# Forget-gate attention: two heads on two halves of TensorE's rows, values token-major, PE's order in blocks

## The chip, the cores and the metric

One core of a Trainium2 chip runs the whole program in one launch. The metric is the device time of an execution in microseconds. Engines: PE (TensorE) multiplies matrices, DVE (VectorE), ACT (ScalarE) and POOL (GpSimd) work on elements, SP (SyncE) issues most DMAs.

## What is computed

Three transformer layers follow each other on 1024 tokens of width 1024: an attention layer with two kinds of heads, the forget-gate layer that this change is about, and a layer with a gated recurrence, cross attention and experts. Of the forget-gate layer, with 16 heads of width 64:

```python
def fox_layer(x, g_in, w_in, b_f, w_out):
    h = rms_norm(x, g_in)
    q, k, v, f_logit, gate = split_cols(h @ w_in, ODD_SPLITS)   # 1024, 1024, 1024, 16, 1024
    log_cum = jnp.cumsum(jax.nn.log_sigmoid(f_logit + b_f), axis=1)
    o = causal_block_attention(q, k, v, log_cum=log_cum)        # 16 heads of 64
    return x + (o * jax.nn.silu(gate)) @ w_out
# in the attention, for each block of 128 queries:
#   s = q k^T / 8 + log_cum[t] - log_cum[s], masked causally; softmax over s; p @ v
```

All is float32.

## The kernel before

Float32 operands of a projection or a score are split into a high part `hi` in a reduced format (F32R) and the rest `lo`; a product is three matmuls (`mm3`, lines 338 to 343: hi hi, hi lo, lo hi). Transposes and value products run on plain float32.

The forget-gate layer (`fox`, lines 1191 to 1377) works on eight pairs of heads; a pair's 128 columns fill the partitions. `prep(p)` makes the filler units of pair p: a unit is 24 matmuls of 512 tokens with a weight block as stationary operand, two units each for queries, keys, gate, and from pair 2 on values. Values of pairs 0 and 1 are made token-major ahead of the loop (line 1203); those of pairs 2 to 7 come out with features on the partitions, and eight transposes turn each pair's into tokens (lines 1266 to 1278).

Scores: for each head, queries are stored with `hi` on the head's 64 partitions and `lo` on the other 64, and the keys' `hi` and `lo` are each stored twice, on both halves; the copies between halves are DMAs on ACT's queue (lines 1256, 1257). So one matmul over 128 partitions is (hi + lo) times a key part, and two passes make a score.

The attention itself (`causal_attn`, lines 579 to 656) has three stages for each of the 64 (pair, block) tiles n: `soft` (scores into a PSUM bank `ps`, bias and running minimum on DVE in line 600, exponential on ACT in line 606, normalisation on POOL in line 609), `tr` (transposes of P into `pt` banks, copied to `PT` by ACT in line 630) and `pv` (line 644: values as stationary operand, 64 columns, one head on each half of the array's columns and of the PSUM partitions). `pipeline` emits in step t the stages `soft(t+2)`, `tr(t+1)`, `pv(t-2)` and one filler unit, interleaved piece by piece; a few `order` edges keep PE's order near that. Within this, a scheduler that simulates the engines orders the instructions of every engine but SP, whose queue is in program order. In the last pair the filler is the memory projections of a later layer (`k.mem.fill`, line 1902), from step 58 on.

PSUM has eight banks: three `ps` (scores), two `pd` (projections), two `pt` (transposes), one `po` (value products). Most tiles of SBUF come out of 41 slots of 128x1024 float32.

Of the kernel before, what the change touches and what calls it, by code (L numbers as in the profile page):

```python
# [66 lines left out]
ET = mybir.EngineType  # L67
SW_MAN = {ET.SP, ET.PE, ET.DVE, ET.Activation, ET.Pool}
# [30 lines left out]
def prep(inp):  # L99
    a = {k: np.asarray(v) for k, v in inp.items()}  # L100
    A = {}
# [475 lines left out]


def causal_attn(k, st, n, qk, bias, scale, val, done):


    nc = k.nc
    P, PT, po = {}, {}, {}

    def soft(i):
        w = (i + 1) * 128
        for a in range(2):
            sb = k.slot([128, 1024], name="P")
            acc = 1e30
            for c in range(0, w, 512):  # L590
                m = min(512, w - c)
                ps = k.pss()
                passes = qk(a, i, c, m)
                for t, (l, r) in enumerate(passes):
                    ins = nc.tensor.matmul(ps[:, :m], l, r, start=t == 0, stop=t == len(passes) - 1)  # L595
                    if t == 0 and c == 0:
                        k.order(ins, st.get(("T", n + i - 2)))
                for c0, n0, b in bias(a, i, c, m):
                    mx = k.small([128, 1], "m", bufs=12)
                    nc.vector.tensor_tensor_reduce(sb[:, c0:c0 + n0], ps[:, c0 - c:c0 - c + n0], b,  # L600
                                                   -scale, acc, OP.add, OP.min, mx)
                    acc = mx
                if c + 512 < w:
                    yield
            sm = k.small([128, 1], "sum", bufs=8)
            nc.scalar.activation(sb[:, :w], sb[:, :w], AF.Exp, bias=acc, scale=-1.0, accum_out=sm)  # L606
            ri = k.small([128, 1], "rinv", bufs=8)
            nc.vector.reciprocal(ri, sm)  # L608
            nc.gpsimd.tensor_scalar(sb[:, :w], sb[:, :w], ri, 0.0, op0=OP.mult, op1=OP.add)  # L609
            P[i, a] = sb  # L610
            yield

    def tr(i):
        for a in range(2):
            p = P.pop((i, a))
            for c in range(0, i + 1, 4):
                m, q = min(4, i + 1 - c), (i // 2, a, c // 4)
                if q not in PT:
                    PT[q] = k.slot([128, 4, 256], name="PT")
                pt = k.pst()  # L620
                for j in range(m):
                    ins = nc.tensor.transpose(pt[:, j * 128:(j + 1) * 128], p[:, (c + j) * 128:(c + j + 1) * 128],  # L622
                                              k.ident)
                    if a == 0 and c == 0 and j == 0:
                        k.order(ins, st.get(("V", n + i - 2)))
                    st["T", n + i] = ins
                dst = PT[q][:, :m, i % 2 * 128:(i % 2 + 1) * 128]
                src = pt[:, :m * 128].rearrange("p (j n) -> p j n", j=m)
                if (a + c // 4) % 4 < 3:
                    nc.scalar.copy(dst, src)  # L630
                else:
                    nc.vector.tensor_copy(dst, src)
                yield

    def pv(i):
        if i % 4 == 0:
            po[0] = k.pso()
        o, half = po[0], i // 2 + 1
        last = half * 2 - 1
        for j in range(i % 2 * half, (i % 2 + 1) * half):  # L640
            n0 = 128 if j == last else 0
            cols = slice((last - 1) % 4 * 128 + n0, (last % 4 + 1) * 128)
            for a in range(2):
                st["V", n + i] = nc.tensor.matmul(o[a * 64:(a + 1) * 64, cols], val(a, j),  # L644
                                                  PT[i // 2, a, j // 4][:, j % 4, n0:],
                                                  start=j == 0, stop=j == last)
            if j % 4 == 3 or j == last:
                for a in range(2):
                    PT.pop((i // 2, a, j // 4))
            if j % 2:  # L650
                yield
        if i % 4 == 3:
            done(i // 4, o)
        yield

    return soft, tr, pv
# [534 lines left out]
def fox(k, ft, resid, after_tile):  # L1191
# [42 lines left out]
    st, qk, gt, lcb, vt = {}, {}, {}, {}, {}  # L1234
    god = k.dram([8, 128, 1024], "god")

    def prep(p):
        def q_evac(half, ps):
            cols = slice(half * 512, (half + 1) * 512)
            if half == 0:  # L1240
                qk[p] = [[k.slot([128, 1024], F32R, name="st") for _ in range(2)] for _ in range(3)]
            for a in range(2):
                r, o = slice(a * 64, a * 64 + 64), slice(64 - a * 64, 128 - a * 64)
                q = qk[p][0][a]
                nc.scalar.activation(q[r, cols], ps[r, :], AF.Copy, scale=0.125)
                nc.vector.scalar_tensor_tensor(q[o, cols], ps[r, :], 0.125, q[r, cols].bitcast(F32),  # L1246
                                               op0=OP.mult, op1=OP.subtract)

        def k_evac(half, ps):
            cols = slice(half * 512, (half + 1) * 512)  # L1250
            for a in range(2):
                r, o = slice(a * 64, a * 64 + 64), slice(64 - a * 64, 128 - a * 64)
                h, l = qk[p][1][a], qk[p][2][a]
                nc.scalar.copy(h[r, cols], ps[r, :])
                nc.vector.tensor_sub(l[r, cols], ps[r, :], h[r, cols].bitcast(F32))
                k.q.dma_start(out=h[o, cols].bitcast(F32), in_=h[r, cols].bitcast(F32))
                k.q.dma_start(out=l[o, cols].bitcast(F32), in_=l[r, cols].bitcast(F32))
# [8 lines left out]
        def v_evac(half, ps):  # L1266
            if half == 0:
                vt[p] = k.slot([128, 1024], name="vT")
            nc.scalar.copy(vt[p][:, half * 512:(half + 1) * 512], ps)
            if half == 1:  # L1270
                v = V[p] = k.slot([128, 8, 128], name="V")
                for b in range(2):
                    pt = k.pst()
                    for t in range(4):
                        i = b * 4 + t
                        nc.tensor.transpose(pt[:, t * 128:(t + 1) * 128], vt[p][:, i * 128:(i + 1) * 128], k.ident)
                    nc.vector.tensor_copy(v[:, b * 4:(b + 1) * 4, :].rearrange("p a b -> p (a b)"), pt)
                vt.pop(p)

# [5 lines left out]
        ev = [q_evac, k_evac] + ([v_evac] if p >= 2 else []) + [g_evac]  # L1285
        units = []
        for e, i in zip(ev, k.fc[p]):
            units += k.proj_units(ft, i, e, order=st.get(("V", (p - 1) * 8 - 1)))
# [6 lines left out]
    def passes(p):  # L1295
        def f(a, i, c, n):
            qs, h, l = qk[p][0][a], qk[p][1][a], qk[p][2][a]
            q = qs[:, i * 128:(i + 1) * 128]
            return [(q, h[:, c:c + n]), (q, l[:, c:c + n])]
        return f  # L1300

    def bias(p):
        def f(a, i, c, n):
            out = []
            if min(c + n, i * 128) > c:
                out.append((c, min(c + n, i * 128) - c, lcb[p][a][:, c:min(c + n, i * 128)]))
            if c + n == (i + 1) * 128:
                dm = k.small([128, 128], "dm", bufs=3)
                nc.gpsimd.tensor_add(dm, lcb[p][a][:, i * 128:(i + 1) * 128], k.mask)  # L1309
                out.append((i * 128, 128, dm))  # L1310
            return out
        return f

    def val(p):
        if p < 2:
            return lambda a, j: V[0][j // 4][:, j % 4, p * 128 + a * 64:p * 128 + (a + 1) * 64]
        return lambda a, j: V[p][:, j, a * 64:(a + 1) * 64]

    def done(p):
        def f(half, o):  # L1320
            t = k.slot([128, 512], name="go")
            nc.vector.scalar_tensor_tensor(t, o, 0.5, gt[p][:, half * 512:(half + 1) * 512], op0=OP.mult, op1=OP.mult)
            k.q.dma_start(out=god[p, :, half * 512:(half + 1) * 512], in_=t)
        return f
# [7 lines left out]
    def fill(t):  # L1332
        p, i = divmod(t, 8)
        if p >= 7:
            return k.mem.fill(FOX_FILL, t) + [ahead(t - 56)]
        if t < 0:
            return []
# [1601 lines left out]
```

## Time and profile before

| | us |
|---|---|
| three runs, median (lowest to highest) | 2300.29 (2298.59 to 2302.42) |
| the profiled execution | 2301.81 |
| its span | 2300.0 |
| the forget-gate stage in it | about 583 to 1203 |

Times in the profile are microseconds from the span's start unless marked ns. PE is the matmul row and PEld the weight-load row of TensorE; records of matmuls overlap, since each shows its whole way through the array. PEclk is the granted TensorE clock as a share of full speed (2.4 GHz). A releaser behind `<-` is what ended an idle time.

### The profile page before, as it was taken

How to read it: one execution, taken by the hardware profiler on the slowest of the kernel's cores; microseconds unless marked ns; L12 is line 12 of the kernel's file. 1: busy time of each engine (PE TensorE's matmuls, PEld its weight loads, DVE VectorE, ACT ScalarE, POOL GpSimd, SP SyncE). 2: the span in 40 equal slices, each digit the busy share in tenths (PEclk: the TensorE clock that was granted, in tenths of full speed). 3: DMA queues.
4: the chain of work that ended last, by engine and by line, in shares of the span. 5: the costliest groups of instructions: out<-in, count | busy, mean ns of one | idle time of the engine just before them, and what ended most of it. 6: DMA issues, size and time to landing. Idle time of an engine off the chain costs nothing.

```text
span 2300.0 us, 32867 instructions
## 1 busy us (share of the span) xinstructions
PE 2211.1 (96%) x12164; PEld 1757.5 (76%) x12164; DVE 1184.4 (51%) x2892; ACT 960.0 (42%) x2018; POOL 452.6 (20%) x620
## 2 busy tenths in 40 slices
PE   7999999999999999999999999999899999899797
PEld 7888778888877777777788789787577888666564
DVE  6322678834344443444344332687445637766544
ACT  5322667823344444444442221355202122557453
POOL 2000455400122222222310010121001102222121
PEclk9999999999999999999999999999999999999898
DMA  4112221233222211221254221326656124778774
GB/s 165 37 48 99 81 58 38 75 118 104 75 69 72 63 55 60 74 60 56 83 174 147 103 91 47 106 69 216 233 220 259 69 106 176 263 235 293 226 216 165
DMA packets 96515, 282.06 MB, mean 123 GB/s; under 512 B 11980, under 2 KB 25036, under 8 KB 96352
## 3 DMA queue, kind: packets, MB, share of 16 engines
q1 hardware_dynamic: 75616, 225.32, 28.4%
q0 software_dynamic: 6624, 24.12, 4.4%
q10 hardware_dynamic: 14112, 30.48, 4.2%
q8 instruction: 97, 1.59, 0.3%
q14 instruction: 66, 0.54, 0.1%
HBM read 202.73 MB, written 65.62 MB: 117 GB/s over the span
## 4 chain that ended last, share of the span: by engine, by line
PE 85%; DVE 6%; DMA 4%; ACT 3%; issue 2%; SPq 0%; POOL 0%; ACTq 0%; POOLq 0%; DVEq 0%
PE pd L340 15%; PE pd L342 15%; PE pd L341 15%; PE ps L340 4%; PE po L644 4%; PE ps L342 4%; PE ps L341 4%; PE ps L595 3%; PE pt L622 3%; PE pd L2538 2%; PE pd L1902 2%; PE ps L990 2%; PE po L1033 1%; PE pt L1019 1%; PE ps L2562 1%
## 5 line engine op out<-in xcount | busy, mean ns | idle before, releaser
L340 PE MATMUL pd<-fh,wh 128*128 128x512 f32 x880 | 353.5, 402 | 0.6 <-DVE st L1246 0.3
L342 PE MATMUL pd<-fh,wl 128*128 128x512 f32 x880 | 347.9, 395 | 0.5 <-DVE wl L318 0.5
L341 PE MATMUL pd<-fl,wh 128*128 128x512 f32 x880 | 347.4, 395 | 0.0
L340 PE MATMUL pd<-wh,fh 128*128 128x258 f32 (+3 forms) x616 | 203.2, 330 | 2.4 <-DVE n L1436 2.4
L342 PE MATMUL pd<-wh,fl 128*128 128x258 f32 (+3 forms) x616 | 200.9, 326 | 0.0
L341 PE MATMUL pd<-wl,fh 128*128 128x258 f32 (+3 forms) x616 | 200.8, 326 | 0.0
L340 PEld LDWEIGHTS pd<-fh,wh 128*128 128x128 f32 x880 | 165.2, 188 | 43.0 <-issue 7.1
L342 PEld LDWEIGHTS pd<-fh,wl 128*128 128x128 f32 x880 | 165.2, 188 | 40.1 <-issue 2.3
L341 PEld LDWEIGHTS pd<-fl,wh 128*128 128x128 f32 x880 | 165.5, 188 | 34.9 <-issue 0.2
L318 DVE TENSOR_TENSOR wl<-w,wh 128x1024 fp32r<-128x1024 f32 (+5 forms) x92 | 106.8, 1166 | 138.3 <-ACT wh L316 138.3
L316 ACT CAST wh<-w 128x1024 fp32r<-128x1024 f32 (+5 forms) x99 | 97.3, 989 | 139.3 <-PE pd L341 108.2
L630 ACT COPY PT<-pt 128x512 f32<-128x512 f32 (+2 forms) x192 | 86.4, 478 | 139.9 <-PE pt L622 139.4
L609 POOL TENSOR_SCALAR P<-P,rinv 128x256 f32<-128x256 f32 (+7 forms) x128 | 96.1, 751 | 192.3 <-DVE rinv L608 163.3
L606 ACT ACTIVATE P<-P,m 128x256 f32<-128x256 f32 (+7 forms) x128 | 99.6, 778 | 76.7 <-DVE m L600 75.8
L340 PEld LDWEIGHTS pd<-wh,fh 128*128 128x128 f32 x616 | 116.4, 189 | 14.2 <-DVE n L1436 2.8
L341 PEld LDWEIGHTS pd<-wl,fh 128*128 128x128 f32 x616 | 116.3, 189 | 10.6 <-issue 1.0
L342 PEld LDWEIGHTS pd<-wh,fl 128*128 128x128 f32 x616 | 116.3, 189 | 10.2 <-issue 0.2
L1309 POOL TENSOR_TENSOR dm<-lcb,mask 128x128 f32<-128x128 f32 x128 | 60.7, 474 | 282.4 <-DVE m L600 226.3
L595 PE MATMUL ps<-st,st 128*128 128x512 f32 (+3 forms) x384 | 106.9, 372 | 1.2 <-DMA st<-st 0.8
L644 PE MATMUL po<-PT,V 128*64 128x256 f32 (+1 forms) x640 | 96.4, 373 | 0.0
L2420 DVE TENSOR_TENSOR ml<-mw,mh 128x1024 fp32r<-128x1024 f32 x66 | 80.1, 1226 | 29.8 <-ACT mh L2417 15.4
L622 PE MATMUL pt<-ident,P 128*128 128x128 f32 x576 | 88.7, 276 | 2.6 <-POOL P L609 2.4
(513 smaller groups left out, 4721.9 us busy)
## 6 DMA issues: line engine op xcount, KB each, us to landing
mw<-w_moe SPq DMA_DIRECT2D x70, 512.0 KB
w<-o_wc SPq DMA_DIRECT2D x30, 512.0 KB
w<-w_moe SPq DMA_DIRECT2D x26, 512.0 KB
xr<-xs SPq DMA_DIRECT2D x18, 512.0 KB
s<-x_wkv SPq DMA_DIRECT2D x16, 512.0 KB
lcb<-dn SPq DMA_DIRECT2D x16, 512.0 KB
st<-st ACTq DMA_DIRECT2D x64, 128.0 KB
wkd<-kvw SPq DMA_DIRECT2D x32, 256.0 KB
```

The costliest lines, as they stand in the source:

```text
L316: nc.scalar.copy(hi[:, :n], raw[:, :n])
L318: (eng or nc.vector).tensor_sub(lo[:, :n], raw[:, :n], hi[:, :n].bitcast(F32))
L340: first = mm(out, lhs[0], rhs[0], start=start, stop=False)
L341: mm(out, lhs[0], rhs[1], start=False, stop=False)
L342: mm(out, lhs[1], rhs[0], start=False, stop=stop)
L595: ins = nc.tensor.matmul(ps[:, :m], l, r, start=t == 0, stop=t == len(passes) - 1)
L606: nc.scalar.activation(sb[:, :w], sb[:, :w], AF.Exp, bias=acc, scale=-1.0, accum_out=sm)
L609: nc.gpsimd.tensor_scalar(sb[:, :w], sb[:, :w], ri, 0.0, op0=OP.mult, op1=OP.add)
L622: ins = nc.tensor.transpose(pt[:, j * 128:(j + 1) * 128], p[:, (c + j) * 128:(c + j + 1) * 128], k.ident)
L630: nc.scalar.copy(dst, src)
L644: st["V", n + i] = nc.tensor.matmul(o[a * 64:(a + 1) * 64, cols], val(a, j), PT[i // 2, a, j // 4][:, j % 4, n0:], start=j == 0, stop=j == ...
L2420: nc.vector.tensor_sub(W[c][1], raw[c], W[c][0].bitcast(F32))
```

## The change

- Scores: queries and keys keep `hi` and `lo` as whole 128-partition tiles (four tiles for a pair). A score is three passes (hi hi, hi lo, lo hi) on a head's 64 partitions; the passes of the pair's two heads alternate, one on the upper and one on the lower half of the rows, into different PSUM banks. The copies between halves go. A second chunk of the second head takes a `pd` bank.
- Values of pairs 2 to 7 are made token-major too: for two pairs at a time, 256 weight columns as moving operand, `v_unit` with 48 matmuls for two token blocks; four such units for each two pairs, as filler in steps 6 and 7 of pairs 0 to 5. Their transposes go. The weights of a group stay in slots.
- `causal_attn` goes; in the loop PE is in program order too (`FOX_MAN`): per step the value products of tile t-2, the scores of tile t+2, the transposes of tile t+1, then the filler. The other engines' instructions for the softmax stand behind the transposes in the program.

```diff
+FOX_MAN = {ET.SP, ET.PE}
...
+    A["o_wv2"] = np.stack([v[:, c * 256:(c + 1) * 256].reshape(8, 128, 256).transpose(1, 0, 2).reshape(128, 2048) for c in range(1, 4)])
...
-        ch += [q[:, c], kk[:, c]] + ([v[:, c]] if p >= 2 else []) + [gate[:, c]]
+        ch += [q[:, c], kk[:, c], gate[:, c]]
...
         def q_evac(half, ps):
             cols = slice(half * 512, (half + 1) * 512)
             if half == 0:
-                qk[p] = [[k.slot([128, 1024], F32R, name="st") for _ in range(2)] for _ in range(3)]
-            for a in range(2):
-                r, o = slice(a * 64, a * 64 + 64), slice(64 - a * 64, 128 - a * 64)
-                q = qk[p][0][a]
-                nc.scalar.activation(q[r, cols], ps[r, :], AF.Copy, scale=0.125)
-                nc.vector.scalar_tensor_tensor(q[o, cols], ps[r, :], 0.125, q[r, cols].bitcast(F32),
-                                               op0=OP.mult, op1=OP.subtract)
+                qk[p] = [k.slot([128, 1024], F32R, name="qk") for _ in range(4)]
+            h, l = qk[p][:2]
+            nc.scalar.activation(h[:, cols], ps, AF.Copy, scale=0.125)
+            nc.vector.scalar_tensor_tensor(l[:, cols], ps, 0.125, h[:, cols].bitcast(F32), op0=OP.mult, op1=OP.subtract)
...
+    def v_unit(g, x):
+
+        if x % 2 == 0:
+            V.setdefault(g, []).append(k.slot([128, 4, 256], name="V"))
+        ps = k.psd()
+        for t in range(2):
+            for kt in range(8):
+                wh, wl = WV[g][kt // 4]
+                c = slice(kt % 4 * 256, (kt % 4 + 1) * 256)
+                k.mm3(ps[:, t * 256:(t + 1) * 256], ft.stat(2 * x + t, kt), (wh[:, c], wl[:, c]), kt == 0, kt == 7)
+        nc.scalar.copy(V[g][x // 2][:, x % 2 * 2:x % 2 * 2 + 2, :].rearrange("p a b -> p (a b)"), ps)
...
+    def score(n):
+
+        p, i = divmod(n, 8)
+        w = (i + 1) * 128
+        qh, ql, kh, kl = qk[p]
+        ps = {}
+        for c in range(0, w, 512):
+            m = min(512, w - c)
+            for a in range(2):
+                ps[c, a] = k.psd() if c and a else k.pss()
+            for l, r in ((qh, kh), (qh, kl), (ql, kh)):
+                for a in range(2):
+                    h = slice(a * 64, a * 64 + 64)
+                    nc.tensor.matmul(ps[c, a][:, :m], l[h, i * 128:w], r[h, c:c + m], start=l is qh and r is kh, stop=l is ql)
...
+    def turn(n):
+        i, z = n % 8, n // 2
+        for a in range(2):
+            p = P.pop((n, a))
+            for c in range(0, i + 1, 4):
+                m, q = min(4, i + 1 - c), (z, a, c // 4)
+                if q not in PT:
+                    PT[q] = k.slot([128, 4, 256], name="PT")
+                pt = k.pst()
+                for j in range(m):
+                    nc.tensor.transpose(pt[:, j * 128:(j + 1) * 128], p[:, (c + j) * 128:(c + j + 1) * 128], k.ident)
...
+                if (a + c // 4) % 4 < 3:
+                    nc.scalar.copy(dst, src)
...
+            g = p // 2 + 1
+            if p < 6:
+                units[p] += [lambda x=x: v_unit(g, x + p % 2 * 2) for x in range(2)]
+                if p % 2 == 0:
+                    units[p][4] = lambda u=units[p][4]: (u(), v_weights(g))
...
-    pipeline(64, [run(0), run(1), run(2)], FOX_SKEW, fill)
-    for t in range(8 - min(FOX_SKEW), 12):
+    a, b, c = FOX_SKEW
+    with k.tc.manual_schedule(engines=FOX_MAN):
+        for t in range(-a, 64 - c):
+            if 0 <= t + c:
+                outs(t + c)
+            if t + a < 64:
+                score(t + a)
+            if 0 <= t + b < 64:
+                turn(t + b)
+            if t + a < 64:
+                soft(t + a)
+            if t < 64:
+                fill(t)
+            else:
+                weave([ahead(t - 56)])
```

`outs` is the value product of `pv` with the same loops, `soft` the exponential, reciprocal and normalisation as before.

## Rows read from the trace of the kernel before

**Rows 1.** The page: busy time, share of the span and instructions of each engine.

```profile
PE 2211.1 (96%) x12164; PEld 1757.5 (76%) x12164; DVE 1184.4 (51%) x2892; ACT 960.0 (42%) x2018; POOL 452.6 (20%) x620
```

**Rows 2.** Windows: stretch, length, busy us per engine (instructions), PEclk, DMA share, GB/s.

```profile
583.00:1203.00 620.00, 615.95 (x3255) 470.48 (x3253) 266.83 (x865) 282.20 (x587) 156.25 (x256) 1.00 0.25 77
1120.00:1160.00 40.00, 37.90 (x226) 27.65 (x226) 17.06 (x68) 19.01 (x45) 12.88 (x23) 0.96 0.28 96
```

**Rows 3.** Matmuls in 583:1203 by line and shape: count | busy us, mean ns.

```profile
L340 PE MATMUL pd<-fh,wh 128*128 128x512 f32 x480 | 192.7, 401 | 0.3 <-DVE st L1246 0.3
...
L622 PE MATMUL pt<-ident,P 128*128 128x128 f32 x576 | 88.7, 276 | 2.6 <-POOL P L609 2.4 <-ACT PT L630 0.2
L644 PE MATMUL po<-PT,V 128*64 128x256 f32 x512 | 82.6, 395 | 0.0
L595 PE MATMUL ps<-st,st 128*128 128x512 f32 x192 | 63.6, 421 | 0.3 <-DVE m L600 0.3
L1902 PE MATMUL pd<-s,s 128*128 128x256 f32 x128 | 28.9, 380 | 0.0
L644 PE MATMUL po<-PT,V 128*64 128x128 f32 x128 | 21.6, 286 | 0.0
L595 PE MATMUL ps<-st,st 128*128 128x384 f32 x64 | 18.3, 368 | 0.0
L595 PE MATMUL ps<-st,st 128*128 128x256 f32 x64 | 14.8, 314 | 0.0
L595 PE MATMUL ps<-st,st 128*128 128x128 f32 x64 | 14.1, 285 | 0.9 <-DMA st<-st 0.8
L1276 PE MATMUL pt<-ident,vT 128*128 128x128 f32 x48 | 7.2, 272 | 0.0
L340 PE MATMUL ps<-wh,fh 128*128 128x512 f32 x8 | 3.3, 417 | 0.0
...
```

**Rows 4.** Timeline of PE: start us, length us, instruction, records merged.

```profile
905.26 0.39 PE L341 MATMUL pd<-fl,wh 128*128 128x512 f32 x1
...
906.19 0.40 PE L342 MATMUL pd<-fh,wl 128*128 128x512 f32 x1
...
909.64 1.04 PE L622 MATMUL pt<-ident,P 128*128 128x128 f32 x8
```

**Rows 5.** Timeline of PE in a later layer, projections of 258 columns.

```profile
1400.05 0.28 PE L340 MATMUL pd<-wh,fh 128*128 128x258 f32 x1
...
1400.90 0.28 PE L341 MATMUL pd<-wl,fh 128*128 128x258 f32 x1
```

**Rows 6.** Timeline of the weight loads, whole array and column halves.

```profile
902.06 0.30 PEld L595 LDWEIGHTS ps<-st,st 128*128 128x128 f32 x2 [0.38 <-DVE rinv L608]
902.43 0.20 PEld L644 LDWEIGHTS po<-PT,V 128*64 128x64 f32 x4
```

**Rows 7.** Timeline of PE around value products, at two places.

```profile
923.68 0.62 PE L595 MATMUL ps<-st,st 128*128 128x512 f32 x2
924.24 0.86 PE L644 MATMUL po<-PT,V 128*64 128x256 f32 x6
...
650.88 1.08 PE L644 MATMUL po<-PT,V 128*64 128x256 f32 x8
651.89 0.51 PE L595 MATMUL ps<-st,st 128*128 128x256 f32 x2
```

**Rows 8.** Timeline: transposes in a row and the copies out of their banks.

```profile
1131.62 1.09 PE L622 MATMUL pt<-ident,P 128*128 128x128 f32 x8
...
1132.31 1.07 ACT L630 COPY PT<-pt 128x512 f32<-128x512 f32 x2
...
1133.04 0.63 PE L622 MATMUL pt<-ident,P 128*128 128x128 f32 x4 [0.33 <-POOL P L609]
...
1176.97 0.96 PE L622 MATMUL pt<-ident,P 128*128 128x128 f32 x7 [0.20 <-ACT PT L630]
```

**Rows 9.** The page's costliest groups: the exponential.

```profile
L606 ACT ACTIVATE P<-P,m 128x256 f32<-128x256 f32 (+7 forms) x128 | 99.6, 778 | 76.7 <-DVE m L600 75.8
```

More of the change, by code (lines that the diff above doesn't have):

```diff
@@ L576, in run @@
         return max(t.values())
[L579 to L586, printed above, removed]
-        for a in range(2):
[L588 to L656, printed above, removed]
@@ L1264, in l_load @@
                 lcb[p].append(t)
[L1266 to L1278, printed above, removed]
         def g_evac(half, ps):
@@ L1283, in g_evac @@
             k.silu2(gt[p][:, half * 512:(half + 1) * 512], ps)
-        ev = [q_evac, k_evac] + ([v_evac] if p >= 2 else []) + [g_evac]
         units = []
-        for e, i in zip(ev, k.fc[p]):
-            units += k.proj_units(ft, i, e, order=st.get(("V", (p - 1) * 8 - 1)))
+        for e, i in zip([q_evac, k_evac, g_evac], k.fc[p]):
+            units += k.proj_units(ft, i, e)
         if p == 0:
@@ new lines, in val @@
+    def val(p, a, j):
+        c = p % 2 * 128 + a * 64
+        return V[p // 2][j // 4][:, j % 4, c:c + 64]
+    def score(n):
[12 more added lines that the diff above has]
+        for a in range(2):
+            P[n, a] = k.slot([128, 1024], name="P")
+            dm = k.small([128, 128], "dm", bufs=3)
+            nc.gpsimd.tensor_add(dm, lcb[p][a][:, i * 128:w], k.mask)
+            M[n, a] = 1e30
+            for c in range(0, w, 512):
+                m = min(512, w - c)
+                for c0, c1, b in ((c, min(c + m, w - 128), lcb[p][a]), (w - 128, c + m, dm)):
+                    if c1 <= c0:
+                        continue
+                    mx = k.small([128, 1], "m", bufs=12)
+                    nc.vector.tensor_tensor_reduce(P[n, a][:, c0:c1], ps[c, a][:, c0 - c:c1 - c], b if b is dm else b[:, c0:c1],
+                                                   -1.0, M[n, a], OP.add, OP.min, mx)
+                    M[n, a] = mx
@@ new lines, in outs @@
+    def outs(n):
+        p, i = divmod(n, 8)
+        if i % 4 == 0:
+            po[0] = k.pso()
+        o, half = po[0], i // 2 + 1
+        last = half * 2 - 1
+        for j in range(i % 2 * half, (i % 2 + 1) * half):
+            n0 = 128 if j == last else 0
+            cols = slice((last - 1) % 4 * 128 + n0, (last % 4 + 1) * 128)
+            for a in range(2):
+                nc.tensor.matmul(o[a * 64:(a + 1) * 64, cols], val(p, a, j), PT[n // 2, a, j // 4][:, j % 4, n0:],
+                                 start=j == 0, stop=j == last)
+            if j % 4 == 3 or j == last:
+                for a in range(2):
+                    PT.pop((n // 2, a, j // 4))
+        if i % 4 == 3:
@@ L1364, in ahead @@
                     yield
[L1366 to L1367 removed]
+    a, b, c = FOX_SKEW
[11 more added lines that the diff above has]
+                fill(t)
+            else:
+                weave([ahead(t - 56)])
+    for t in range(8 - c, 12):
         for _ in ahead(t):
```

82 lines of the change are left out of this document (33 added, 49 removed).

## The prediction

> **What bounds the kernel now.** Read the page's busy shares first: TensorE (PE) is busy 96% of the span, the next engine 51% [rows 1]. Then the windows over the stage that the change rewrites, from the first query projection of the forget-gate layer to the first output projection after its last value product: 620.0 us long, PE busy 615.95, granted clock 1.00, DMA 25% busy, VectorE (DVE) 267 us and ScalarE (ACT) 282 us busy [rows 2]. So in this stage time is what PE's instructions take one after another, and an edit is worth what it takes off PE's row; DVE, ACT and DMA work counts only where PE ends up waiting for it.
>
> How much of the 620 is arithmetic? The counts of each shape are in [rows 3]; "busy" there overlaps (a matmul's record lasts longer than its turn on the array), so I price by start-to-start distance. Projections of 512 columns: four apart in 0.93 us, 0.2325 each; transposes: eight in 1.04 with the last record's 0.27 taken off, 0.110 each [rows 4]. A 258-column matmul: seven apart in 0.85, 0.121 [rows 5]; I use it for 256 columns, and midway, 0.176, for 384. Weight loads: two in 0.30, each 0.19 long, so they start 0.11 apart; a 128-column score can't go faster than its load, 0.109 [rows 6]. Value products of two heads lie side by side on the two column halves: eight records in 1.08, less the last record's 0.38 and a first load of 0.05, are three distances for four pairs, 0.216 a pair of 256 columns [rows 7]. The sums:
> - projections 3 x 480 x 0.2325 = 334.8, and 22 of the output projection that the scheduler already put here, 5.1
> - transposes (576 + 48) x 0.110 = 68.6
> - value products 256 pairs x 0.216 + 64 x 0.108 = 62.2
> - scores 192 x 0.2325 + 64 x (0.176 + 0.121 + 0.109) = 70.6
> - the memory projections (L1902) 128 x 0.216 = 27.6
>
> Together 568.9. The other 51.1 us are the loss. 4.05 is idle PE (620.0 less 615.95). Most of the rest is changing between the whole array and column halves. Two 512-column scores ahead of a value block take 0.56 where 0.465 is due: 0.09 to enter. Eight records take 1.01 to the next instruction where 0.865 is due: 0.146 inside and on leaving. The next matmul then waits for its load, 0.107 [rows 6, 7]. One visit costs 0.34, the timeline of the stage has 100 of them (650.88 and 924.24 are two), so 34. The last 13 are blocks in which one head stands alone, and a clock dip.
>
> **The change, part by part.**
>
> *Scores.* Per chunk and pair of heads: before, two heads x two passes, four matmuls on 128 rows; after, three passes x two heads on 64 rows each, in adjacent instructions and separate PSUM banks. If the halves run side by side as the column halves do, a chunk costs three turns and not four: 70.6 x 3/4 = 52.9, a gain of 17.6. No 64-row matmul is in the trace. Bounds: 17.6 gained, or, if the halves take turns, six turns for four, 35.3 lost. I take the gain, by the nearest row: in column mode four weight loads fit in 0.20 at 0.13 each [rows 6], and the value blocks run at a pair per 0.216 [rows 7].
>
> *Values token-major.* Out: 12 units x 24 x 0.2325 and 48 transposes x 0.110, 72.2. In: 12 units x 48 matmuls of 256 columns x 0.121 = 69.7. Gain 2.5. Between the 256-column price and the 258-column row there is hardly room: 1 either way.
>
> *PE's order by mode.* Each step now is value products, scores, transposes, filler, so three mode changes: into columns 0.09, inside and out 0.146, load for the rows 0.107, out of the rows 0.095 and first transpose 0.055 (as for columns), 0.49 a step, 64 steps, 31.4. It replaces the whole 51.1. The rows show the price for columns only; for rows it may be nothing (0.15 a step less) or a little more.
> The Trainium skill (TensorEngine Tiling (Array Packing), Key Properties) says that changing the tiling mode drains TensorE and changing the tile within a mode does not. By it all three changes cost, and the sum stands; the trace agrees for whole-array to column changes (0.34 a visit) and can't speak of rows.
>
> *New waits, because PE's order is fixed.* Before, the scheduler put projections between the transposes of a tile; after, all transposes of a tile stand together, and scores, filler and everything else on PE queue behind them. From the fifth tile of a pair on there are four groups (4 + m of the first head, then the second), only two PSUM banks, and every copy out of them is on ACT. Eight transposes start at 1131.62, the first copy at 1132.31, the third group at 1133.04: 1.42 later, 1.36 without the slow first one; 0.73 after the copy began, which is one copy and 0.14. That row names POOL as releaser, but the row at 1176.97 shows the same wait with ACT's copy named [rows 8]. The first two groups fill 0.55, 0.66, 0.77 and 0.88 (m = 1 to 4, 0.110 each), so PE waits 0.81, 0.70, 0.59, 0.48: 2.58 a pair of heads, 20.6 in eight pairs. Bounds: 10 if half is hidden, 50 if copies come late (a rival below).
>
> *Steps without filler.* In 1120 to 1160, where before's filler ran out for two steps, PE idles 2.10 and the clock falls to 0.96 of 40 us, 1.6 more [rows 2]. After, the value units sit in pairs 0 to 5, so two more steps lack filler, and at the start the first transposes wait for the first softmax with nothing between: I put 7.6 (twice 3.7, rounded up) in place of it. Other small waits: 3, a guess between 0 and 10.
>
> *Costed at nothing:* the 64-row splits on ACT and DVE become half as many 128-row ones, 64 small copies between halves and their issues on ACT's queue go, 12 copies of value transposes go; all lay behind PE. The value weights come as six slot pieces instead of six of the 30 blocks on SP's queue, the same bytes; at 25% DMA they stay hidden. The row broadcasts keep their place in SP's queue. Without PE as cover the weight splits would show: that happens only in the steps just priced. The 22 output-projection matmuls can't be drawn forward any more and come later, which the sum holds as 5.1 on both sides.
>
> *Sum for the stage:* 568.9 - 17.6 - 2.5 + 31.4 + 20.6 + 7.6 + 3 = 611.4, against 620.0: 8.6 less. The profiled execution took 2301.81 us (1.8 more than its span); the median of the runs is 2300.29, 1.5 lower. 2301.8 - 8.6 - 1.5 = 2292.
>
> **The rivals.**
>
> (a) *The row halves cost no drain.* 0.15 x 64 = 9.6 less: 2282. For it: transposes and projections follow each other with no loss, so not every change of shape costs. Against: the column change does.
>
> (b) *The two halves share their weight load.* Each pair then lasts at least two loads, 0.215: +0.039, +0.094, +0.106 for 384, 256 and 128 columns, x 3 passes x 2 chunks x 8 = 11.5 more: 2303.5, no change. For it: whole-array loads stand 0.11 apart; against: column loads go side by side [rows 6].
> The Trainium skill (TensorE: Matmul & The Clock Gate, Part 3: Packing small matmuls, Measured speedup vs the span model) reports 3.07 times, not 4, for four strips of rows at 512 columns. An estimate from that page: two halves gain 1.54, not 2, scores come to 68.8 and the time to 2308. No run here shows it yet.
>
> (c) *The halves don't run together at all*, so the change doesn't do what it says. 52.9 more than forecast: 2345, slower. It decides from where a pair costs more than 1.16 turns (8.6 of 52.9). Against it stand the column pairs.
>
> (d) *Copies behind exponentials.* PE can't go round a late copy now. An exponential takes 0.78 on ACT [rows 9]. If in half of the 64 steps one stands ahead of the first copy, 32 x 0.78 = 25 more: 2317, slower. It decides from twelve such steps on. For it: ACT is in order and its order was not fixed by hand. Against it: the copies stand before the exponentials in the program, and ACT is under half busy.
>
> **How the numbers follow.** Forecast 0.48 (own range 2283 to 2303), (a) 0.12, (b) 0.15, (c) 0.08, (d) 0.17. Runs of this kernel lie within 0.2%, about 4.6 us, of each other; a smaller change can't be told. Faster (below 2295.7): 0.35 out of the forecast's 0.48, all of (a), 0.01 of (b): 0.48. Same: 0.13 of the forecast and 0.08 of (b): 0.21. Slower: (c), (d) and the last 0.06 of (b): 0.31. The range for 8 in 10 runs from 2277 (a with fewer small waits) to 2325 (d and 8 us of small waits), and leaves out (c) and the far side of (d).
>
> **What would show it right or wrong.** Scores: adjacent 64-row records of the two heads starting within 0.01 us, pairs 0.23 apart at 512 columns; (b) shows as 0.215 at 128 columns, (c) as 0.23 between heads. Values: 0.121 a matmul. Modes: three losses of 0.09 to 0.15 in each step, 64 value blocks and not 100. Banks: PE idle 0.5 to 0.8 before the third group of transposes of tiles 5 to 8 of a pair, released by ACT's copy; (d) shows as idles over 1 us with an exponential between. Idle in the stage should go from 4 to about 30 us while PE's arithmetic falls by 20. A stage under 600 or over 625 us would mean that one of these terms is not as I have it; PE waiting for POOL's normalised tiles in steps with filler would mean a wait that I left out.

## The result, and the profile after

The changed kernel took 2317.81 us (2315.77 to 2318.90, four runs) against 2299.86 for the kernel before beside it (2298.59 to 2302.42, four): a ratio of 1.0076, 95% interval 1.0058 to 1.0093. The change costs 0.8%, 18 us; the forecast was 9 us less. The profiled execution took 2315.77, its span 2314.0, 14.0 more than before's.

The page's busy shares, to be read beside [rows 1]:

```profile
PE 2190.0 (95%) x12596; PEld 1750.0 (76%) x12596; DVE 1152.9 (50%) x2848; ACT 940.6 (41%) x1986; POOL 451.7 (20%) x620
```

PE does 21 us less work and DVE and ACT 31.5 and 19.4 less, yet the time is longer. Windows over the rewritten stage and inside it (columns as in [rows 2]):

```profile
582.00:1220.00 638.00, 599.51 (x3705) 467.05 (x3704) 234.68 (x820) 261.02 (x553) 152.98 (x256) 0.98 0.18 62
...
670.00:674.80 4.80, 0.10 (x1) 0.00 (x0) 4.17 (x11) 1.62 (x3) 0.00 (x0) 0.99 0.67 211
674.80:678.00 3.20, 3.15 (x11) 2.88 (x12) 1.57 (x5) 2.26 (x4) 0.00 (x0) 0.50 0.97 351
```

From its first projection (582.3) to the first output projection after its last value product (1219.8) the stage lasts 637.6, against 620.2. PE's busy time fell by 16 [rows 2]; its idle time rose from 4 to 38.5. The lower lines show one such place: PE stands still for almost 5 us, and in the 3.2 us behind that its granted clock is 0.50, the lower of its two levels (1.2 GHz). Who made it wait, summed over the stage (line waited for, us in total, times, longest):

```profile
PE pt L1265 <- ACT PT L1269: 28.6, 30, 4.8
PE ps L342 <- DVE m L1242: 6.1, 1, 6.1
PE pt L1265 <- POOL P L1253: 3.5, 3, 2.6
```

Transposes (L1265) waited for ScalarE's copies out of their banks (L1269). The 30 waits are of two kinds: 27 of 0.33 to 0.71 us, and three of 4.75. This is the first of the three, in pair 0: PE's timeline, then that of ScalarE, of VectorE and of the load queue (ACTq and SPq issue DMAs):

```profile
666.40 0.40 PE L344 MATMUL pd<-fh,wl 128*128 128x512 f32 x1
666.73 0.87 PE L1283 MATMUL po<-PT,V 128*64 128x256 f32 x8
667.53 1.20 PE L1230 MATMUL ps<-qk,qk 64*128 64x512 f32 x7
...
668.57 0.39 PE L1230 MATMUL ps<-qk,qk 64*128 64x512 f32 x1
668.57 0.39 PE L1230 MATMUL pd<-qk,qk 64*128 64x512 f32 x1
668.80 0.38 PE L1230 MATMUL ps<-qk,qk 64*128 64x512 f32 x1
668.80 0.38 PE L1230 MATMUL pd<-qk,qk 64*128 64x512 f32 x1
669.12 0.98 PE L1265 MATMUL pt<-ident,P 128*128 128x128 f32 x7
674.85 1.73 PE L1265 MATMUL pt<-ident,P 128*128 128x128 f32 x7 [4.75 <-ACT PT L1269]
676.23 0.78 PE L342 MATMUL pd<-fh,wh 128*128 128x512 f32 x1
...
678.34 0.40 PE L344 MATMUL pd<-fh,wl 128*128 128x512 f32 x1
```

```profile
667.39 1.99 ACT L318 CAST wh<-w 128x1024 fp32r<-128x1024 f32 x2
671.45 0.34 ACTq L1292 DMA_DIRECT2D god<-go  x1
673.17 1.04 ACT L318 CAST wh<-w 128x1024 fp32r<-128x1024 f32 x1 [3.80 <-DMA w<-o_wc]
674.13 0.96 ACT L1269 COPY PT<-pt 128x512 f32<-128x512 f32 x2
```

```profile
668.46 2.36 DVE L320 TENSOR_TENSOR wl<-w,wh 128x1024 fp32r<-128x1024 f32 x2 [0.25 <-ACT wh L318]
670.74 0.68 DVE L1291 SCALAR_TENSOR_TENSOR go<-po,gt 128x512 f32<-128x512 f32 x1
```

```profile
669.71 1.46 SPq L282 DMA_DIRECT2D w<-o_wc  x2
```

The first bank could be copied from about 669.9 on (0.75 after its first transpose, as in the rows at 728.53 and 729.28 below). But ScalarE, which works in the order of its queue, had two things ahead of the copies. One is the store of the gated output, which waits for VectorE; VectorE had first to split two value weights (668.46 to 670.7), so the store goes out at 671.45. The other is the cast of a query weight that only the *next* pair's filler needs: its load could be issued at 669.71 only, when the first split had freed a raw buffer (there are two), and landed at 673.17. The copies start at 674.13. PE, whose order is fixed, has a filler that is ready and may not take it up. The same happens in pairs 2 and 4, the other two in which value weights are split.

What was forecast of PE's own work can be read in the same lines. The two heads' matmuls start together (668.57 and 668.57; 285 pairs of records are 3 ns apart in the median) and pairs follow each other 0.23 apart.

The Trainium skill (TensorE: Matmul & The Clock Gate, Part 3: Packing small matmuls, Measured speedup vs the span model) has 3.07 times for four strips of rows, from which I had estimated 1.54 for two halves. This trace doesn't bear that estimate out: at 512 columns a pair of halves takes the 0.23 of one whole matmul.

Into columns: 0.33 from 666.40 to 666.73 where 0.23 is due. Inside and out of columns: 0.80 to 667.53 where 0.65 is due (two pairs at 0.216, two of half the columns). In and out of rows: 1.59 for six pairs to 669.12 where 1.40 is due. Together 0.44 a step; 0.49 was forecast.

The counts, beside [rows 3] (as there: count | busy us, mean ns):

```profile
L342 PE MATMUL pd<-wh,fh 128*128 128x256 f32 x192 | 54.9, 286 | 0.0
...
L1230 PE MATMUL ps<-qk,qk 64*128 64x512 f32 x264 | 44.2, 423 | 0.0
...
L342 PE MATMUL ps<-wh,fh 128*128 128x512 f32 x13 | 6.1, 471 | 6.1 <-DVE m L1242 6.1
```

The last line is the output projection: 12 of these 13 records, with their two partners 36 matmuls and 8.4 us, stand inside the stage. And an ordinary bank wait, at tile 6 of pair 1 (PE, then ScalarE), which answers to [rows 8]:

```profile
728.53 0.77 PE L1265 MATMUL pt<-ident,P 128*128 128x128 f32 x5
730.01 0.74 PE L1265 MATMUL pt<-ident,P 128*128 128x128 f32 x5 [0.71 <-ACT PT L1269]
```

```profile
729.28 0.75 ACT L1269 COPY PT<-pt 128x512 f32<-128x512 f32 x2 [1.61 <-PE pt L1265]
```

Five transposes are worth 0.55 of PE's time and the next comes 1.48 after the first: the wait costs 0.9, more than its idle of 0.71, since the last record before it runs on for 0.16 after its turn on the array (it lasts 0.27, a turn 0.11).

### The profile page after: what moved, and what is told of

The parts are those of the page before. It is cut to its first block, busy times and chain, and to the rows that moved or that the text cites. A ratio compares the mean times of both kernels' runs of the same rounds, so it can differ in the third digit from the quotient of the medians.

```text
span 2314.0 us, 33469 instructions
## 1 busy us (share of the span) xinstructions
PE 2190.0 (95%) x12596; PEld 1750.0 (76%) x12596; DVE 1152.9 (50%) x2848; ACT 940.6 (41%) x1986; POOL 451.7 (20%) x620
## 5 line engine op out<-in xcount | busy, mean ns | idle before, releaser
L342 PE MATMUL pd<-fh,wh 128*128 128x512 f32 x784 | 317.6, 405 | 0.3 <-ACT u L1371 0.2
L344 PE MATMUL pd<-fh,wl 128*128 128x512 f32 x784 | 309.9, 395 | 0.5 <-DVE wl L320 0.5
L343 PE MATMUL pd<-fl,wh 128*128 128x512 f32 x784 | 309.1, 394 | 0.0
L342 PE MATMUL pd<-wh,fh 128*128 128x256 f32 (+3 forms) x808 | 257.3, 319 | 1.2 <-DVE n L1417 1.2
L344 PE MATMUL pd<-wh,fl 128*128 128x256 f32 (+3 forms) x808 | 254.8, 315 | 0.0
L343 PE MATMUL pd<-wl,fh 128*128 128x256 f32 (+3 forms) x808 | 254.3, 315 | 0.0
L343 PEld LDWEIGHTS pd<-wl,fh 128*128 128x128 f32 x808 | 152.4, 189 | 10.7 <-issue 1.0
L344 PEld LDWEIGHTS pd<-wh,fl 128*128 128x128 f32 x808 | 152.2, 188 | 10.1 <-issue 0.2
L1269 ACT COPY PT<-pt 128x512 f32<-128x512 f32 (+2 forms) x192 | 84.6, 481 | 126.4 <-PE pt L1265 123.8
L1265 PE MATMUL pt<-ident,P 128*128 128x128 f32 x576 | 86.6, 287 | 32.2 <-ACT PT L1269 28.6
L1242 DVE CUSTOM_DVE_ANT_0 P<-ps,lcb 128x512 f32<-128x512 f32 (+3 forms) x112 | 64.0, 572 | 92.5 <-PE ps L1230 92.4
L1265 PEld LDWEIGHTS pt<-ident,P 128*128 128x128 f32 x576 | 63.3, 144 | 53.5 <-issue 43.6
L1253 POOL TENSOR_SCALAR P<-P,rinv 128x256 f32<-128x256 f32 (+7 forms) x128 | 95.9, 752 | 38.3 <-DVE rinv L1252 19.4
```

What stands on the lines that cost most here:

```text
L342: first = mm(out, lhs[0], rhs[0], start=start, stop=False)
L343: mm(out, lhs[0], rhs[1], start=False, stop=False)
L344: mm(out, lhs[1], rhs[0], start=False, stop=stop)
L1242: nc.vector.tensor_tensor_reduce(P[n, a][:, c0:c1], ps[c, a][:, c0 - c:c1 - c], b if b is dm else b[:, c0:c1], -1.0, M[n, a], OP.add, OP.m ...
```

## The experiments

**What PE may do while it waits.** Theory: the waits cost because the blocked transposes stand ahead of a filler of the same mode that is ready.

```
-                turn(t + b)
+                turn(t + b, (0,))
 ...
                 fill(t)
+            if 0 <= t + b < 64:
+                turn(t + b, (1,))
```

> The changed kernel with only PE's fixed order altered: the filler (24 matmuls, 5.6 us, the same mode as transposes) stands between the first head's transposes and the second head's, ScalarE's queue as it was. Theory (PE pays only because nothing that is ready may pass the blocked transposes): the 31 bank waits (0.33 to 0.71 us, 16 us in all) and the three waits of 4.75 us vanish behind the filler, with their half-clock stretches: 16 + 14 + 4.5 less than 2317.8, about 2283; the tail's 6.1 us stays or goes: 2276 to 2285. Rival (copies late by more than the filler, exponentials ahead): the idle comes back behind the filler, 2300 or more.

Measured 2281.34, ratio to before 0.9926 (0.9909 to 0.9942): faster than before, and 36 us less than the changed kernel (35 by the two ratios). PE's waits in its stage:

```profile
PE pt L1265 <- POOL P L1253: 8.4, 6, 2.6
PE ps L342 <- DVE m L1242: 2.9, 1, 2.9
PE pt L1265 <- ACT PT L1269: 0.6, 1, 0.6
```

The waits for copies went from 28.6 to 0.6. ScalarE's order was not touched, and the cast still stands ahead of the copies; it no longer reaches PE. Three new idles of 1.35 to 1.85 us stand a tile later, before transposes that wait for GpSimd.

**What makes the copies late.** First ScalarE's queue: the casts of weights behind the latest copies, then also the store. Both runs split the next query weight earlier in the program as well, in the second value unit, so that the late cast doesn't come too late for its own use.

```
+            self.order(ins, self.behind)      # ins: the cast; behind: the latest copy
 ...
+            k.order(k.q.dma_start(out=god[p, :, cols], in_=t), k.behind)     # second run only
 ...
```

> The changed kernel with one thing moved: ScalarE's casts of the attention weights stand behind the latest copies of transposed tiles in its queue (and the next pair's query weight is cast two steps earlier, so that nobody waits for it). Theory (ScalarE's in-order queue: in three steps PE idles 4.75 us before its third group of transposes, because the copies stand behind a wait for the store of a gated output, until 671.45 in the first of them, and then behind a cast that waits for its weight to land, until 674.13): the second half of that wait goes, about 2.7 us in each of three steps, and some of the half-clock stretch behind it: 8 to 11 us less than the changed kernel's 2317.8, so 2307 to 2310. Rival 1 (the weights themselves come too late, so PE would wait for them a little further on): 2316 to 2319. Rival 2 (prediction's (d): exponentials ahead of copies): no change, 2318.

> As before, and the store of the gated output is issued from ScalarE's queue after the step's copies. Theory: the three idles of 4.75 us become the ordinary bank wait of 0.44 us, and the three stretches at half clock behind them go (about 1.5 us each): 17 us less than 2317.8, so about 2300, as the kernel before. Rival (the order on ScalarE's queue is not it; the fixed order on PE costs what it costs): 2315 to 2319.

Measured 2310.66 (ratio 1.0042, 1.0027 to 1.0057), at the upper end of the theory's 2307 to 2310: the waits fell from 4.75 to 2.45. With the store behind as well 2306.37 (1.0032, 1.0020 to 1.0043), 6 us short of the theory's 2300: the three waits are down to 0.44, but 1.5 to 1.9 us of idle stand a tile later, before the transposes of the pair's last tile, and up to 0.84 right behind; both wait for GpSimd. The order of ScalarE's queue is a part of it; something else is late too.

The same from PE's side, the filler put between the heads' transposes in these three steps only:

```
-                turn(t + b)
+                turn(t + b, (0,) if t + b in (6, 22, 38) else (0, 1))
 ...
+            if t + b in (6, 22, 38):
+                turn(t + b, (1,))
```

> The changed kernel with the filler between the two heads' transposes in three of the 64 steps only, those in which PE idles 4.75 us; the other 61 as they were, so the ordinary bank waits stay. Theory (these three waits and the half-clock stretches behind them are 3 x (4.75 + 0.16 + about 1.5) = 19 us, the ordinary bank waits the rest of what the filler between them gained): 2298 to 2301, against 2317.8 for the changed kernel and 2281.3 with the filler between in every step. Rival (most of that gain came from the bank waits): 2308 or more. Rival 2 (the late copies only meet the next block): 2312 or more.

Measured 2313.9 (1.0056, 1.0037 to 1.0074): my theory of 2300 failed. The time fits both rivals (2308 or more, 2312 or more); the trace speaks for the second: the three long waits for copies are gone, and new ones of 1.8 to 3.4 us, each with one of 0.83 behind it, stand a tile later before transposes that wait for GpSimd. PE after the filler, then GpSimd (POOL), which normalises the tiles that PE transposes, and the load queue:

```profile
675.28 0.93 PE L1265 MATMUL pt<-ident,P 128*128 128x128 f32 x7
...
679.92 1.09 PE L1265 MATMUL pt<-ident,P 128*128 128x128 f32 x8 [1.79 <-POOL P L1253]
681.85 1.54 PE L1265 MATMUL pt<-ident,P 128*128 128x128 f32 x6 [0.83 <-POOL P L1253]
```

```profile
678.32 0.45 POOL L1234 TENSOR_TENSOR dm<-lcb,mask 128x128 f32<-128x128 f32 x1 [13.16 <-DMA lcb<-dn]
678.75 1.12 POOL L1253 TENSOR_SCALAR P<-P,rinv 128x1024 f32<-128x1024 f32 x1
```

```profile
669.48 1.46 SPq L282 DMA_DIRECT2D w<-o_wc  x2
671.04 1.93 SPq L1179 DMA_DIRECT2D lcb<-dn  x2
```

It is the same pattern on another engine. GpSimd has a mask addition for the next pair's first tile ahead of the normalisation of the last tile's P, and that addition waits for the pair's row broadcast, issued at 671.04 behind two weights and there at 678.3. In the changed kernel the same addition stood until 678.77 behind the same load; PE, itself 4.75 us later, did not meet it:

```profile
678.77 0.46 POOL L1234 TENSOR_TENSOR dm<-lcb,mask 128x128 f32<-128x128 f32 x1 [13.38 <-DMA lcb<-dn]
```

So the delay should have a source before any engine's order: in one step two value weights and a query weight are cast and split through two raw buffers, and loads of 512 KB each, weights and broadcasts, follow each other (DMA share 0.97 in the last of the windows above). The test takes this lump apart and orders nothing on ScalarE or GpSimd:

```
-    def v_weights(g):
-        WV[g] = [k.w_get(i, 0) for i in k.fv2[g]]
+    def v_weight(g, x):
+        WV.setdefault(g, []).append(k.w_get(k.fv2[g][x], 0))
 ...
-                    units[p][4] = lambda u=units[p][4]: (u(), v_weights(g))
+                    for x in range(2):
+                        units[p][3 + 2 * x] = lambda u=units[p][3 + 2 * x], x=x: (u(), v_weight(g, x))
```

> The changed kernel with the two value weights of a pair split two steps apart (in its fourth and sixth step) in place of both in the fifth. Theory (the three idles of 4.75 us come from the lump: two value weights and the next query weight are cast, split and loaded one behind the other through two raw buffers, so the third is not there when its cast stands ahead of the copies; moved behind the copies, the lump delays the next small tile's exponentials): with the lump taken apart neither wait is left, 3 x (4.75 + 0.16 + about 1.5 of half clock) = 19 us: 2298 to 2302. Rival 1 (the ScalarE and VectorE work of these weights is too much for the stretch wherever it stands): 2308 to 2314, as with the filler in three steps. Rival 2 (a load that stands behind others on the queue, whatever the order): 2315 to 2319.

Measured 2300.39 (1.0007, 0.9998 to 1.0017), as the theory has it. The same place on ScalarE and on GpSimd, and PE's waits in the stage:

```profile
670.18 0.34 ACTq L1292 DMA_DIRECT2D god<-go  x1
671.20 0.97 ACT L1269 COPY PT<-pt 128x512 f32<-128x512 f32 x2 [2.37 <-PE pt L1265]
```

```profile
675.68 1.96 POOL L1234 TENSOR_TENSOR dm<-lcb,mask 128x128 f32<-128x128 f32 x2 [8.02 <-DMA lcb<-dn]
```

```profile
PE pt L1265 <- ACT PT L1269: 16.2, 31, 0.8
PE ps L342 <- DVE m L1242: 6.3, 1, 6.3
PE pt L1265 <- POOL P L1253: 3.8, 4, 2.6
```

ScalarE now waits for PE and not the other way about, and the broadcast is there at 675.7 in place of 678.8; no wait for a copy is longer than 0.8, and no idle has come in their place. The 16.2 left are the ordinary bank waits. So 16 of the 18 us by which the change was slower (the two ratios, 1.0076 and 1.0007) came from the step in which the value weights are split.

The edit moves something on SP's queue too: the broadcasts now stand behind one weight and not two, and the first of them is issued at 656.69 already. The second, issued at 671.60, no earlier than in the changed kernel, is there 4.1 us later; in the changed kernel 7.5 us pass from the first issue (671.27) to the addition. How much of the broadcasts' part comes from their place and how much from the fewer loads beside them is not told apart.

**The tail.** The wait of 6.1 stands near 1187, in the last pair, where pieces of the attention's output are loaded and split. The test stands on the run with casts and store behind, so it is to be compared with 2306.37 and not with the changed kernel.

```
-                    k.split(hi, lo, t)
+                    k.order(nc.scalar.copy(hi, t), k.behind)
+                    nc.vector.tensor_sub(lo, t, hi.bitcast(F32))
```

> As the one before, and the casts of the loaded output pieces in the last pair stand behind the copies as well. Theory: PE's idle of 6.11 us near 1187 goes and 1.4 us of half clock with it: 7.5 us less than the run with casts and store behind, about 2293. Rival (those pieces are late because only one input buffer is free, so PE pays later, in the output projection): no change against it, 2300.

Measured 2312.03 (1.0059, 1.0042 to 1.0076), where 2293 was expected: a miss, and not faster than the run it stands on. The wait is still there, 6.3 us. The edit didn't reach it: the cast that waits belongs to the step before and was ordered behind that step's copies only. The load queue shows why its piece is late: the second of two loads issued together waits for one of the three input buffers, two of which hold the pair's row broadcasts:

```profile
1159.50 11.69 SPq L1339 DMA_DIRECT2D gor<-god  x2
```

Loading one piece a step, and splitting it a step later, took the wait away, there with the filler between (below).

**Whether row halves run together, and what the fixed order is worth.** Two runs: the passes of one head, then those of the other; and PE's order left to the scheduler.

```
-            for l, r in ((qh, kh), (qh, kl), (ql, kh)):
-                for a in range(2):
+            for a in range(2):
+                for l, r in ((qh, kh), (qh, kl), (ql, kh)):
```

> The changed kernel with the two heads' scores no longer alternating: the three passes of one head, then the three of the other, on the same row halves. Theory (adjacent matmuls on different halves run together, and PE issues in order): only the last pass of the first head and the first of the second can overlap, five turns a chunk for three, 52.9 x 5/3 = 88: 35 us more, 2345 to 2355. Rival (each half of the rows keeps its own queue and the order of issue doesn't matter): 2316 to 2319. Prediction's (c), halves never together, would have shown as this price already in the changed kernel.

```
-FOX_MAN = {ET.SP, ET.PE}
+FOX_MAN = {ET.SP}
```

> The changed kernel with PE's order in this stage left to the scheduler again, everything else (row-half scores, token-major values) kept. Theory (the arithmetic is 20 us less, but each return to the scheduler's order brings the mode changes back: about 100 column visits at 0.34 as before and as many row visits at about 0.2, 54 us against 51 us of loss in the kernel before): 20 us gained, 3 to 20 lost, and no wait of PE behind blocked transposes: 2280 to 2300, so less than the 2317.8 of the fixed order. Rival (the fixed order is what makes row halves pay, the free one splits the pairs of heads apart or multiplies the visits): over 2318.

Heads in turn: 2324.18 (1.0113, 1.0092 to 1.0134; two runs), 6 us more than the changed kernel (8.5 by the ratios) and not 35. The score blocks take 68.7 us in all, 69.0 in the changed kernel. Though three matmuls of one head and then three of the other are issued, the halves still run side by side, 0.01 us apart:

```profile
668.25 0.39 PE L1230 MATMUL ps<-qk,qk 64*128 64x512 f32 x1
668.25 0.39 PE L1230 MATMUL pd<-qk,qk 64*128 64x512 f32 x1
668.48 0.38 PE L1230 MATMUL ps<-qk,qk 64*128 64x512 f32 x1
668.49 0.38 PE L1230 MATMUL pd<-qk,qk 64*128 64x512 f32 x1
```

Of the us that it is longer, 4.1 are new waits of projections for a `pd` bank that VectorE has not emptied yet (L1167 makes the low part of the queries); the scores' second head holds such a bank:

```profile
PE pd L342 <- DVE qk L1167: 4.1, 7, 0.6
```

Why they come with this order was not followed. The free order took 2308.68 (1.0046, 1.0029 to 1.0063), above my 2280 to 2300 and below the rival's 2318. To the next layer's first projection it changes mode 262 times (196 with the fixed order), leaves 92 of 576 score matmuls without their partner beside them, so that the score blocks take 77.7, and idles 13.7 us instead of 40.8. So the fixed order does what it is for: it saves 66 changes and 9 us of split pairs. In the changed kernel its waits cost more than that.

**Putting it together.** With the filler between, the first filler ahead of the second tile's transposes and one output piece a step:

> The run with the filler between the two heads' transposes (2281.3), with two waits taken away: the first filler stands ahead of the second tile's transposes (idle 2.63 us near 623 and about 1.4 us of half clock), and in the last pair each output piece is loaded one step before it is split, one a step, so that no cast waits for its load (idle 2.89 us near 1155). Theory: 5 to 7 us less, 2274 to 2277. Rival (the tail's pieces only move the wait into the output projection, and the start's wait moves to the next tile): 2280 to 2283.

Measured 2275.62 (0.9897, 0.9879 to 0.9915), as expected. Then the value products of two tiles in every second step:

```
-            if 0 <= t + c:
+            if 0 <= t + c and t % 2 == 0:
                 outs(t + c)
+                outs(t + c + 1)
```

> As the one before, and the value products of two tiles stand together in every second step (one column visit for two). Theory (each change of mode costs about 0.1 us, and a visit 0.05 inside): in every two steps one change and one such start fewer, 32 x 0.15 = 5 us less than the run before. Rival (changes within a step cost nothing once the next loads are queued): no change against it.

Measured 2266.98 (0.9870, 0.9852 to 0.9887), and again 2267.13 beside the next kernels: 8.6 less for 32 changes of mode fewer (196 to 164), more than the 5 expected. But three idles also shrank (1.7 to 2.5 us before, 1.0 to 1.3 after), and two stretches of some 3.3 us at half clock behind them went, so the price of a change of mode can't be read from this time.

> The same kernel as the run with values merged, beside the one above on the same chip: 2265 to 2269 if nothing but the kernel decides.

> The fastest run so far (filler between, first filler early, output pieces one step ahead, value products merged: 2267.0) and with it the casts of weights and the stores behind the copies on ScalarE's queue. Theory (three idles of about 1.1 us stand where a small tile's exponentials come late behind casts): 3 to 5 us less, 2262 to 2264. Rival (as in the run with casts and stores behind and no filler between, the wait only moves to the next tile, by way of VectorE): 2266 to 2269.

The kernel of that last run lacked three of its edits (first filler early, pieces one step ahead, values merged). Its 2277.71 (0.9902, 0.9888 to 0.9916) is the time of the filler between with casts and stores behind; it says nothing on what it was to tell apart. The run that was meant, and beside it the lump taken apart on the fastest kernel:

> The fastest run so far with casts and stores behind the copies, which an earlier run was to show (the kernel of that run had neither the early first filler, nor the output pieces one step ahead, nor the merged values: its time of 2277.7 stands for the filler between with casts and stores behind, against 2281.3 without). Theory of the lump: the order on ScalarE only moves the wait, 2264 to 2268; were the order the cause: 2262 to 2264.

> The fastest run so far (2267.0: filler between, first filler early, output pieces one step ahead, values merged) with the value weights apart as well. Theory of the lump: its three idles of about 1.1 us with their slow clock go, 3 to 6 us less: 2261 to 2264. Rival: 2266 to 2269.

Casts behind: 2263.87 (0.9848, 0.9833 to 0.9863), at the top of what one theory expected (2262 to 2264) and just under the other (2264 to 2268). Lump apart: **2262.09** (0.9836, 0.9822 to 0.9849), 1.6% less than the kernel before and the lowest time of all. Against 2267 without either, both gains are 3 to 5 us. Once PE has the filler to do, either remedy serves, and the two times don't tell them apart. The traces do: with the casts behind, idles of 0.9 us are left at the ends of two pairs, before transposes that wait for GpSimd, whose mask addition waits for the broadcast as before; with the lump apart there is none up to the last pair. The stage of the second, to be read beside the first window of the changed kernel, and PE's waits in it:

```profile
582.00:1166.00 584.00, 580.87 (x3701) 466.80 (x3701) 237.51 (x822) 264.20 (x556) 155.64 (x256) 1.00 0.20 68
```

```profile
PE pt L1266 <- POOL P L1254: 1.3, 2, 0.9
PE pd L1903 <- DMA s<-x_wkv: 0.8, 1, 0.8
PE pt L1266 <- ACT PT L1270: 0.6, 1, 0.6
```

PE is busy but for 3 us, at full clock throughout.

## Why the prediction was wrong

*Scores: right.* The pairs are 0.235, 0.175, 0.119 and 0.112 apart in the median for 512, 384, 256 and 128 columns; 144 and 48 of each make 53.3 us, 52.9 forecast. That rules out rivals (b), which wanted 0.215 a pair at 128 columns, and (c), which wanted 0.23 between the two heads. *Values: right* (0.118 a matmul in the trace, 0.121 forecast). *Modes: right*, 0.44 a step for 0.49, and rows cost as columns do, which rules out rival (a).

The Trainium skill (TensorEngine Tiling (Array Packing), Key Properties) says that a change of mode drains TensorE. The trace agrees, for rows too: each of the three changes of a step costs about 0.1 us.

*Bank waits: right.* In the changed kernel 27 idles of 0.33 to 0.71 us behind ScalarE's copies add up to 14.3; with the tail of 0.16 behind each, as in the row at 730.01, they are 18.6, where 20.6 was forecast for 32 (in three of those places the long waits stand instead, and the last pair's last two tiles do not wait).

*The step that failed* is the paragraph "Costed at nothing", where it says of the value weights that they are "the same bytes; at 25% DMA they stay hidden". Over the stage the DMA share is 0.18; but at the first of the three places it is 0.67 while PE stands still and 0.97 in the 3.2 us behind, and ScalarE's cast waits 3.80 us for a weight, so in these steps the loads are not hidden. What I did not ask is what two splits in one step do to the raw buffers, to VectorE, and to ScalarE's and GpSimd's queues, on which the copies and tiles that PE waits for also stand. Three waits of 4.75 us, and the half clock behind each, are 19 us by the rows; taking the lump apart gave 16 to 17.

*The second miss* is of the same kind, the tail: 6.1 us, which the last pair's loaded pieces cost, is not in the sum; 7.6 was put there for the start and for steps without filler, and 3 for small waits. What came was 2.63 at the start and 6.1 in the tail, 0.16 more for each, and half clock: after the 4.75 us the seven transposes take 1.38 (674.85 to 676.23) where 0.77 is due and the five projection matmuls behind them 2.11 (to 678.34) where 1.16 is due, 1.5 more; about the same at the start and in the tail. Long waits and their clock are 23.0 of idle, 0.8 and 7.6, together 31, where 10.6 stood. That is 20 or 21 of the 26 us by which the stage (637.6) exceeds the sum (611.4). Another 3.3 is no loss: 36 matmuls of the output projection stand in the stage, and not the 22 of before, which the prediction said could not be drawn forward. Net, some 2 us are left. But the changes of mode came out 3 us cheaper than forecast and the value units 1.7, so the losses whose place is not known are nearer 7; 16 small matmuls that the sum does not list (L1144, 0.11 each) are 1.7 of them.

*Rival (d)* gave 2317, and its place was right (ScalarE's in-order queue, with a fixed PE order that can't go round); its cause was not. In the changed kernel only one of the waits for a copy (at 1141.2, 0.56 us) has an exponential right ahead of that copy, which makes it less than 0.25 longer; the exponential itself is as long as before [rows 9]. What stood ahead were a store and a cast, in three steps and not in 32. The time matched by accident.

With the value weights two steps apart the kernel takes 2300.39, no less than the kernel before. Less the tail's 6.3 and its 1.4 of half clock that would be 2292.7, as forecast, but no run has these two edits alone, and errors of several us in both directions stand in that sum.

## What to carry to other kernels

Where an engine's order is fixed by hand, every wait on its path has to be walked through on the *other* engines' queues, with what those have to do in that very step: what a load, a split and a store do there counts by their place and not by their bytes or the mean share of use. Put work that is ready, and needs no change of mode, between two dependent blocks rather than behind both: here that was worth some 35 us, more than the change itself was to bring. And work that comes in lumps (weights for the next group) is better spread by a step or two: moving it in one queue, or letting one engine pass it, left part of the wait to the next engine that takes its instructions in order.

## What the runs showed of the hardware that was not expected

Matmuls on the two row halves don't have to be issued alternately. Issued as three of one half and three of the other, they still start in pairs, 0.01 us apart (some 280 pairs) instead of 0.003, and the score blocks take the same time (68.7 us and 69.0). In the changed kernel, after 2.6 to 6.1 us without a matmul the granted clock was at the lower level for about 3 us of work in each of the five places; behind the idles under 1 us the matmuls kept their distances. For lengths between these, the length of an idle does not settle it: with the casts alone behind, three idles of 2.4 to 2.5 us left the granted clock at 1.00, and with one output piece a step idles of 1.95 and 1.68 us were followed by 3.3 us at 0.50, one of 2.54 was not.
